# Two chained matrix products with a gelu: zeros from a constant, a cast on two engines, and one matmul moved ahead of two transposes

## The chip, the cores and the metric

The kernel runs on one core of one Trainium2 chip. The metric is the time on the device in microseconds (us); lower is better. A core has TensorE (PE: matrix products and transposes; its weight loads are listed as PEld), VectorE (DVE), ScalarE (ACT) and GpSimd (POOL). SyncE (SP) and POOL also issue transfers (DMA) between HBM and the on-chip memory SBUF. TensorE writes into PSUM, eight banks of 128 partitions x 2 KB. The four runs of the kernel before took 117.74, 118.13, 118.16 and 119.73 us, median 118.15.

## The reference

```python
m, k, n, p = 1024, 1024, 2048, 1024          # all float32
h = np.matmul(a, b)                          # a: m x k, b: k x n
h = 0.5 * h * (1 + np.tanh(np.sqrt(2 / np.pi) * (h + 0.044715 * h ** 3)))
return np.matmul(h, c).astype(np.float32)    # c: n x p
```

## The kernel before, in words

The instructions of each engine stand in the order in which the code writes them; a recording layer adds the waits for data and buffers, per tile. So the order of the calls is the order of the work.

**Data.** `a` is needed with k on the partitions, so it is transposed on TensorE. It is cut into two halves of 512 rows (h = 0 upper, 1 lower) and four quarters of 256 columns of k (q = 0 to 3). A quarter of a half is 128 x 4 x 256 numbers. The upper q = 0 and q = 1 and the lower q = 0 come in float32 over SP into `sta` and are cast to bf16 on the chip (`cast_a` into `ab`, a tile with two buffers). The other five are cast by the transfer itself, which POOL issues (`cast_load_a` into `abq`). `b` is cut into eight slices of 128 rows of k: slices 0 and 1, columns 0 to 511, come in float32 into `stb` and are cast by `cast_b` into `b1`; the rest of `b`, and all of `c`, come over POOL with the cast in the transfer. POOL's first transfer waits for a one-column copy (`gate`, L81) that reads the first quarter of `a`, so its queue starts only when that has landed. POOL issues slices 2 and 3 of `b`, the lower q = 1 of `abq`, the upper q = 2, slices 4 and 5, the lower q = 2, and so on.

**The first product** makes hidden columns 0 to 511 in the plain way, the transposed result in PSUM: bank t (`ps[0, t]`) holds 128 hidden columns by the 512 upper rows, `ps[1, t]` the same for the lower rows. `block(h, tiles, ks)` issues one 128x512 matmul for each slice and tile (L114).

**A turn** (`turn(h, q, bank, ab)`, L136) transposes one quarter of one half: two times four 128x128 transposes into one PSUM bank (L143), each four followed by a VectorE copy into `aT` (L144), which gives the slices 2q and 2q + 1 of that half. It is a generator: each `next(tn)` issues one half of it, so that matmuls can be put between the halves. Both halves lie in one tile `pt`, so the second half's transposes wait until the copy of the first is done. (`turn(1, 0)` alone uses two banks.)

**Stirs** (`stir`, L122) are matmuls of zeros from the tile `warm` into a bank that is overwritten later. They only keep TensorE busy. VectorE sets `warm` to zero at the start (L50). Being float32, each stir is two passes in the trace.

**The order at the start** (L225 to L262): four stirs of 256 columns; the upper q = 0 is cast on VectorE and turned, with a stir of 256 between the halves and one of 128 behind; `cast_b` casts slice 0 in two halves and slice 1, all on ACT; the upper half's matmuls of slice 0 (four) and two of slice 1; `turn(1, 0)`; the two left of slice 1; three matmuls of slice 0 for the lower half (three tiles only, since a bank is needed for the turns); `turn(0, 1)` with three more between its halves. Then for q = 1 and 2 the loop of L249: the upper half's four matmuls of slice 2q and one of slice 2q + 1, the first half of the lower turn `turn(1, q)`, the other three matmuls, its second half; then the lower half's three matmuls, and the upper `turn(0, q + 1)` with three matmuls between its halves. `zero.t1` is a VectorE difference of upper and lower `aT` (one slice at a time here), needed later.

**What follows**, untouched by the change: the gelus (L118, on ACT), three more groups of seven instead of eight block products for the rest of the first product and for the second one (`seven`, L302, its matmuls at L208), and the stores over SP.

Of the kernel before, what the change touches and what calls it, by code (L numbers as in the profile page):

```python
# [9 lines left out]
F32 = mybir.dt.float32  # L10
F32R = mybir.dt.float32r
BF16 = mybir.dt.bfloat16
AF = mybir.ActivationFunctionType
# [6 lines left out]
def kernel(ctx, tc, a, b, c, out):  # L20
    nc = tc.nc
# [3 lines left out]
    H = 512  # L25
# [8 lines left out]
    consts = ctx.enter_context(tc.tile_pool(name="consts", bufs=1))  # L34
# [5 lines left out]
    def slot(tag, shape, dt, name):  # L40
        return big.tile(shape, dt, name=name, tag=tag)

    def bank(i, shape=(128, H), dt=F32, name="ps"):
        return pp.tile(list(shape), dt, name=name, tag=f"bank{i}", padded_shape=None)

    def pieces(tag, bufs, shape, dt, name):
        return small.tile(shape, dt, name=name, tag=tag, bufs=bufs)

    warm = consts.tile([128, 256], F32, name="warm")
    nc.vector.memset(warm, 0.0)  # L50
    ident = consts.tile([128, 128], BF16, name="ident")
    make_identity(nc, ident)
    gate = consts.tile([128, 1], F32, name="gate")
# [7 lines left out]
    b1 = slot("b1", [128, KT, 1024], BF16, "b1")  # L61
# [4 lines left out]
    stb = slot("x0", [128, KT, H], F32, "stb")  # L66
# [39 lines left out]
    def copy(eng, dst, src):  # L106
        if eng is nc.scalar:
            nc.scalar.activation(dst, src, AF.Copy)
        else:
            nc.vector.tensor_copy(dst, src)  # L110

    def mm1(p, t, h, ks):
        for k in ks:
            nc.tensor.matmul(p, b1[:, k, ts(t, 128)], aT[:, h, k],  # L114
                             start=(k == 0), stop=(k == KT - 1))
# [6 lines left out]
    def stir(*widths):  # L122

        for w in widths:
            nc.tensor.matmul(ps[0, 3][:, 0:w], warm[:, 0:128], warm[:, 0:w],
                             start=True, stop=True, skip_group_check=True)

    def cast_a(h, q, *engs):

        ab = pieces("ab", 2, [128, 4, 256], BF16, "ab")  # L130
        for i, eng in enumerate(engs):
            w = 256 // len(engs)
            copy(eng, ab[:, :, ts(i, w)], sta[:, h, q][:, :, ts(i, w)])
        return ab

    def turn(h, q, i, ab):  # L136

        banks = i if isinstance(i, tuple) else (i,)
        pts = [bank(x, (128, 2, H), BF16, "pt") for x in banks]
        for n in range(2):  # L140
            pt = pts[n % len(pts)]
            for m in range(4):
                nc.tensor.transpose(pt[:, n, ts(m, 128)], ab[:, m, ts(n, 128)], ident)  # L143
            nc.vector.tensor_copy(aT[:, h, 2 * q + n], pt[:, n])  # L144
            yield

    def cast_b(k, n=1):
        for i in range(n):
            r = ds(i * (H // n), H // n)
            nc.scalar.activation(b1[:, k, r], stb[:, k, r], AF.Copy)  # L150

    def block(h, tiles, ks):
        for k in ks:
            for t in tiles:
                mm1(ps[h, t], t, h, (k,))
# [56 lines left out]
    def pair(i):  # L212
        x = slot(f"x{i}", [128, 2, 4, H], F32R, "x1")
        return x[:, 0], x[:, 1]
# [3 lines left out]
    def quarters(b, c0, w):  # L218
        return [[b[:, 0:4, ds(c0, w)], b[:, 4:8, ds(c0, w)]],
                [b[:, 0:4, ds(c0 + w, w)], b[:, 4:8, ds(c0 + w, w)]]]  # L220

    zero = Seven(4, quarters(b1, H, 256), BB, [None] * 4, [None] * 4, 2)
    one = Seven(4, quarters(b2, 0, H), BB, [None] * 4, zero.t)

    stir(256, 256, 256, 256)  # L225
    tn = turn(0, 0, 4, cast_a(0, 0, nc.vector))
    next(tn)
    stir(256)
    next(tn)
    stir(128)  # L230
    cast_b(0, 2)
    cast_b(1)
    ab = cast_a(1, 0, nc.vector, nc.scalar)
    block(0, range(4), (0,))
    block(0, range(2), (1,))
    for _ in turn(1, 0, (7, 6), ab):
        pass
    ab = cast_a(0, 1, nc.scalar, nc.scalar)
    block(0, range(2, 4), (1,))
    for t in range(3):  # L240
        ps[1, t] = bank(4 + t)
    zero.t[0], zero.t[1] = pair(2)
    zero.t1(4, 0)
    block(1, range(3), (0,))
    tn = turn(0, 1, 7, ab)
    next(tn)
    block(1, range(3), (1,))
    next(tn)
    for q in range(1, 3):  # L249
        k = 2 * q  # L250
        block(0, range(4), (k,))
        block(0, range(1), (k + 1,))
        tn = turn(1, q, 7, abq[:, q, 1])
        next(tn)
        block(0, range(1, 4), (k + 1,))
        next(tn)
        zero.t1(4, q)
        block(1, range(3), (k,))
        tn = turn(0, q + 1, 7, abq[:, q + 1, 0])
        next(tn)  # L260
        block(1, range(3), (k + 1,))
        next(tn)  # L262
# [221 lines left out]
```

## Time and profile before

| what | us |
|---|---|
| median of four runs | 118.15 |
| the profiled execution's own time | 118.16 |
| its span in the profile | 116.4 |
| PE busy | 111.3 |
| DVE busy | 89.2 |
| ACT busy | 51.8 |
| POOL busy | 17.5 |
| stirs at L125, first start and length of the eight passes | 1.19, 3.77 |
| first transposes (L143) | 5.24 |
| first matmul of a block (L114) | 7.02 |
| first matmul of L208 in the final unbroken run of 400 | 25.16 |

The profile is of one execution. Its span runs from the first to the last recorded instruction; the time of the execution is 1.8 us longer, because of what lies around it. "L125" is line 125 of the kernel before. A busy TensorE is not TensorE at its peak: matmuls are pipelined, and the length of a group includes the drain of its last one, so the pace is read from the starts. In the time line a row is: start, length, engine, line, operation, result and operands, shapes, count, and in brackets the idle time of that engine before it with what ended it. In the chain of waits a row is: start, length, what the end of the program hung on at that time.

### The profile page before, as it was taken

Reading aid. Unit: us, or ns where it says so; the run is one execution under the profiler, and the core shown is the slowest. Engines: PE = TensorE matmul, PEld = TensorE weight load, DVE = VectorE, ACT = ScalarE, POOL = GpSimd, SP = SyncE. Lnnn points to the kernel's source line nnn. Section 1 sums busy time; section 2 is a strip of 40 time slices with the busy share of each in tenths; the row PEclk is TensorE's granted clock in tenths of the full one; section 3 lists DMA queues with packets and bytes.
Section 4 is the critical chain, followed back from the end, with each engine's and each line's share of the span. In section 5 each row is a group of like instructions: output and inputs, shape, how many; then the busy total and the mean of one; then the engine's idle time right before and its main releaser. Section 6 shows DMA issues by size and latency. Waiting matters only on the chain.

```text
span 116.4 us, 1453 instructions
## 1 busy us (share of the span) xinstructions
PE 111.3 (96%) x540; PEld 76.3 (66%) x540; DVE 89.2 (77%) x104; ACT 51.8 (44%) x86; POOL 17.5 (15%) x29
## 2 busy tenths in 40 slices
PE   5999999999999999999999999999999999999980
PEld 4545455545777447888886444588888888888860
DVE  0246356799998999744689999999999986954670
ACT  5063000799369998066699329600033982000000
POOL 2498555222332000000000000000000000000000
PEclk9999999999999999999999999999999999999999
DMA  2999999999999999999000000070000002014993
GB/s 65 307 357 160 200 198 207 201 207 207 206 208 211 212 210 213 210 211 184 8 0 0 0 6 0 2 268 0 0 0 0 0 0 96 0 63 176 367 366 109
DMA packets 13542, 15.81 MB, mean 136 GB/s; under 512 B 736, under 2 KB 9696, under 8 KB 13536
## 3 DMA queue, kind: packets, MB, share of 16 engines
q0 software_dynamic: 8800, 9.44, 48.3%
q1 hardware_dynamic: 4736, 6.29, 15.2%
q8 instruction: 4, 0.07, 0.2%
q14 instruction: 2, 0.02, 0.0%
HBM read 20.97 MB, written 4.19 MB: 216 GB/s over the span
## 4 chain that ended last, share of the span: by engine, by line
PE 86%; DMA 9%; POOL 1%; DVE 0%; issue 0%
PE ps L208 76%; PE ps L114 8%; DMA abq<-in_a_dram 6%; DMA sta<-in_a_dram 3%; PE pt L143 2%; POOL b L89 1%; POOL gate L81 1%; DVE ot L371 0%
## 5 line engine op out<-in xcount | busy, mean ns | idle before, releaser
L208 PE MATMUL ps<-x,s 128*128 128x512 f32 x128 | 29.6, 391 | 0.0
L208 PEld LDWEIGHTS ps<-x,s 128*128 128x128 f32 x128 | 24.0, 188 | 5.1
L208 PE MATMUL ps<-x,x 128*128 128x512 f32 x96 | 22.8, 393 | 0.0
L208 PEld LDWEIGHTS ps<-x,x 128*128 128x128 f32 x96 | 18.0, 188 | 3.9
L114 PE MATMUL ps<-aT,b 128*128 128x512 bf16 x64 | 16.1, 379 | 0.2 <-ACT b L150 0.2
L294 ACT ACTIVATE v<-ps 128x512 f32<-128x512 f32 x10 | 6.0, 599 | 19.5 <-PE ps L208 19.5
L208 PE MATMUL ps<-c_sb,hT 128*128 128x512 bf16 (+1 forms) x72 | 14.2, 356 | 0.0
L208 PE MATMUL ps<-x 128*128 128x512 f32 x56 | 13.2, 392 | 0.0
L144 DVE COPY aT<-pt 128x512 bf16<-128x512 bf16 x16 | 6.7, 423 | 7.0 <-PE pt L143 7.0
L118 ACT ACTIVATE hT<-ps 128x512 bf16<-128x512 f32 x14 | 7.3, 596 | 10.5 <-PE ps L114 10.5
L208 PEld LDWEIGHTS ps<-x 128*128 128x128 f32 x56 | 10.2, 188 | 2.6 <-ACT v L294 0.4
L208 PEld LDWEIGHTS <-hT 128*128 128x128 bf16 x72 | 6.9, 98 | 7.0 <-issue 0.5
L118 ACT ACTIVATE hT<-ot 128x512 bf16<-128x512 f32 x18 | 10.5, 625 | 1.4 <-DVE ot L299 1.2
L208 PE MATMUL ps<-aT,b 128*128 128x512 bf16 x48 | 10.7, 379 | 0.0
L299 DVE TENSOR_TENSOR ot<-ps,v 128x512 f32<-128x512 f32 x10 | 6.7, 687 | 5.2 <-DMA out_dram<-ot 3.8
L299 DVE TENSOR_TENSOR ot<-ps,u 128x512 f32<-128x512 f32 x10 | 6.7, 689 | 5.1 <-ACT u L294 5.1
L166 DVE TENSOR_TENSOR x<-c_sb 128x1024 fp32r<-128x1024 bf16 x8 | 9.2, 1214 | 0.0
L114 PEld LDWEIGHTS <-b 128*128 128x128 bf16 x64 | 5.5, 97 | 4.9 <-ACT b L150 0.9
L208 PEld LDWEIGHTS <-b 128*128 128x128 bf16 x48 | 4.6, 98 | 5.7 <-issue 0.3
L104 POOL DMA_DIRECT2D c_sb<-in_c_dram x8 | 5.7, 712 | 12.5 <-DMA b<-in_b_dram 11.8
L294 ACT ACTIVATE u<-ps 128x512 f32<-128x512 f32 x10 | 5.9, 596 | 3.3 <-PE ps L208 3.2
L166 DVE TENSOR_TENSOR x<-b 128x1024 fp32r<-128x1024 bf16 (+1 forms) x4 | 7.0, 1751 | 0.2 <-issue 0.2
(43 smaller groups left out, 109.5 us busy)
## 6 DMA issues: line engine op xcount, KB each, us to landing
c_sb<-in_c_dram POOLq DMA_DIRECT2D x8, 512.0 KB, 19.7
b<-in_b_dram POOLq DMA_DIRECT2D x6, 512.0 KB, 15.0
out_dram<-ot SPq DMA_DIRECT2D x12, 256.0 KB, 2.1
sta<-in_a_dram SPq DMA_DIRECT2D x3, 512.0 KB, 6.1
abq<-in_a_dram POOLq DMA_DIRECT2D x5, 256.0 KB, 8.5
out_dram<-ot SPq DMA_DIRECT2D x8, 128.0 KB, 2.0
b<-in_b_dram POOLq DMA_DIRECT2D x3, 256.0 KB, 7.9
stb<-in_b_dram SPq DMA_DIRECT2D x1, 512.0 KB, 5.3
```

The source lines that it names most:

```text
L81: nc.gpsimd.tensor_copy(gate, sta[:, 0, 0, 3, 0:1])
L89: nc.gpsimd.dma_start(out=b1[:, 2 * q:2 * q + 2, 0:H], in_=b_part(q))
L104: nc.gpsimd.dma_start(out=c_sb[:, t:t + 2], in_=cv[:, t:t + 2])
L114: nc.tensor.matmul(p, b1[:, k, ts(t, 128)], aT[:, h, k], start=(k == 0), stop=(k == KT - 1))
L118: nc.scalar.activation(hT[h][:, t], p, AF.Gelu_apprx_tanh)
L143: nc.tensor.transpose(pt[:, n, ts(m, 128)], ab[:, m, ts(n, 128)], ident)
L144: nc.vector.tensor_copy(aT[:, h, 2 * q + n], pt[:, n])
L166: nc.vector.tensor_tensor(out=dst[:, r], in0=x[:, r], in1=y[:, r], op=op)
L208: nc.tensor.matmul(p[:, ds(c0, w)], l[:, k, ts(j, 128)], r[:, k, ds(c0, w)], start=(start and k == 0), stop=(k == self.kt - 1), skip_group ...
L294: nc.scalar.activation(st, p, AF.Copy)
L299: nc.vector.tensor_tensor(out=ot, in0=p, in1=st, op=ADD)
```

## The change

The tile `warm` goes; the zeros are a constant that the program's preamble writes into SBUF, one number per partition, read as 128x256 with no step between elements. There are five stirs of 256 at the start instead of four, the one between the halves of the first turn is 128 columns wide instead of 256, and the one behind it 64 instead of 128. `cast_b` takes the engines: slice 0 is cast by halves on VectorE and ACT, with VectorE's half ahead of the copy of the first turn's second half; slice 1 stays on ACT. Three instead of two matmuls of slice 1 stand ahead of `turn(1, 0)`, and one behind it. The upper q = 1 is cast by halves on ACT and VectorE instead of twice on ACT. One matmul of slice 1 for the lower half moves ahead of `turn(0, 1)`. The first `zero.t1` moves behind that turn. In the loop, two instead of one matmul of slice 2q + 1 stand ahead of the lower turn, and two instead of three between its halves. One source line less: lines from L51 on are one lower in the changed kernel until L223.

```diff
-    warm = consts.tile([128, 256], F32, name="warm")
-    nc.vector.memset(warm, 0.0)
+    warm = nc.const_aps.tensor(0.0, [128, 256], F32)
...
-    def cast_b(k, n=1):
-        for i in range(n):
-            r = ds(i * (H // n), H // n)
-            nc.scalar.activation(b1[:, k, r], stb[:, k, r], AF.Copy)
+    def cast_b(k, *engs):
+        w = H // len(engs)
+        for i, eng in enumerate(engs):
+            copy(eng, b1[:, k, ts(i, w)], stb[:, k, ts(i, w)])
...
-    stir(256, 256, 256, 256)
+    stir(256, 256, 256, 256, 256)
     tn = turn(0, 0, 4, cast_a(0, 0, nc.vector))
     next(tn)
-    stir(256)
-    next(tn)
     stir(128)
-    cast_b(0, 2)
-    cast_b(1)
+    cast_b(0, nc.vector, nc.scalar)
+    next(tn)
+    stir(64)
+    cast_b(1, nc.scalar)
     ab = cast_a(1, 0, nc.vector, nc.scalar)
     block(0, range(4), (0,))
-    block(0, range(2), (1,))
+    block(0, range(3), (1,))
     for _ in turn(1, 0, (7, 6), ab):
         pass
-    ab = cast_a(0, 1, nc.scalar, nc.scalar)
-    block(0, range(2, 4), (1,))
+    block(0, (3,), (1,))
+    ab = cast_a(0, 1, nc.scalar, nc.vector)
     for t in range(3):
         ps[1, t] = bank(4 + t)
     zero.t[0], zero.t[1] = pair(2)
+    block(1, range(3), (0,))
+    block(1, range(1), (1,))
+    tn = turn(0, 1, 7, ab)
+    next(tn)
+    block(1, range(1, 3), (1,))
+    next(tn)
     zero.t1(4, 0)
-    block(1, range(3), (0,))
-    tn = turn(0, 1, 7, ab)
-    next(tn)
-    block(1, range(3), (1,))
-    next(tn)
     for q in range(1, 3):
         k = 2 * q
         block(0, range(4), (k,))
-        block(0, range(1), (k + 1,))
+        block(0, range(2), (k + 1,))
         tn = turn(1, q, 7, abq[:, q, 1])
         next(tn)
-        block(0, range(1, 4), (k + 1,))
+        block(0, range(2, 4), (k + 1,))
         next(tn)
         zero.t1(4, q)
```

More of the change, by code (lines that the diff above doesn't have):

```diff
@@ L223 @@
     one = Seven(4, quarters(b2, 0, H), BB, [None] * 4, zero.t)
-    stir(256, 256, 256, 256)
+    stir(256, 256, 256, 256, 256)
     tn = turn(0, 0, 4, cast_a(0, 0, nc.vector))
     next(tn)
-    stir(256)
+    stir(128)
+    cast_b(0, nc.vector, nc.scalar)
     next(tn)
-    stir(128)
-    cast_b(0, 2)
-    cast_b(1)
+    stir(64)
+    cast_b(1, nc.scalar)
     ab = cast_a(1, 0, nc.vector, nc.scalar)
     block(0, range(4), (0,))
-    block(0, range(2), (1,))
+    block(0, range(3), (1,))
     for _ in turn(1, 0, (7, 6), ab):
         pass
-    ab = cast_a(0, 1, nc.scalar, nc.scalar)
-    block(0, range(2, 4), (1,))
+    block(0, (3,), (1,))
+    ab = cast_a(0, 1, nc.scalar, nc.vector)
     for t in range(3):
@@ L242 @@
     zero.t[0], zero.t[1] = pair(2)
-    zero.t1(4, 0)
     block(1, range(3), (0,))
+    block(1, range(1), (1,))
     tn = turn(0, 1, 7, ab)
     next(tn)
-    block(1, range(3), (1,))
+    block(1, range(1, 3), (1,))
     next(tn)
+    zero.t1(4, 0)
     for q in range(1, 3):
```

## The prediction

> **What bounds the kernel now.** I read the busy line first, then the chain of waits, then the time line of the head, engine by engine. The busy line says which engine to follow; TensorE works 96% of the span, so only its idle time can be won and any new idle time of it is lost.
>
> ```profile
> PE 111.3 (96%) x540; PEld 76.3 (66%) x540; DVE 89.2 (77%) x104; ACT 51.8 (44%) x86; POOL 17.5 (15%) x29
> ```
>
> The chain of waits (start, length, what) says from where on that holds. Up to 12.77 us it consists of transfers: the first quarter of `a`, the gate on POOL, then the cast-load of `abq`, issued at 5.99 and landed at 12.73. From there it is TensorE alone until two output additions.
>
> ```profile
> 0.74 3.73 DMA sta<-in_a_dram
> ...
> 5.99 6.73 DMA abq<-in_a_dram
> 12.73 0.05 issue
> 12.77 0.40 PE pt L143 x4
> 13.17 0.65 PE ps L114 x3
> ...
> 25.16 87.99 PE ps L208 x400
> ```
>
> So there are two regions. Ahead of 12.77 an instruction matters only if it makes TensorE come to the transposes of `turn(1, 1)` after the data. Behind 12.77 each idle stretch of TensorE moves the end. The time line of TensorE (start, length, what) shows the border and the two lower turns:
>
> ```profile
> 11.37 1.25 PE L114 MATMUL ps<-aT,b 128*128 128x512 bf16 x5
> 12.77 0.40 PE L143 MATMUL pt<-ident,abq 128*128 128x128 bf16 x4
> 13.01 0.81 PE L114 MATMUL ps<-aT,b 128*128 128x512 bf16 x3
> 13.69 0.38 PE L143 MATMUL pt<-ident,abq 128*128 128x128 bf16 x4
> ...
> 15.74 1.24 PE L114 MATMUL ps<-aT,b 128*128 128x512 bf16 x5
> 16.82 0.39 PE L143 MATMUL pt<-ident,abq 128*128 128x128 bf16 x4
> 17.04 0.81 PE L114 MATMUL ps<-aT,b 128*128 128x512 bf16 x3
> 17.72 0.38 PE L143 MATMUL pt<-ident,abq 128*128 128x128 bf16 x4
> ```
>
> A length includes the drain of the last instruction, so I take spacings: a 128x512 matmul comes every (1.25 - 0.38)/4 = 0.22 us, a transpose every (0.40 - 0.23)/3 = 0.06 us (0.38 and 0.23 are single ones). Five matmuls from 11.37 are issued by 12.46, so TensorE waits 0.31 us for `abq` at 12.77. At 16.82 it doesn't wait: five matmuls from 15.74 end at 16.82. VectorE's copies in the same stretch:
>
> ```profile
> 13.21 0.42 DVE L144 COPY aT<-pt 128x512 bf16<-128x512 bf16 x1 [1.34 <-PE pt L143]
> ...
> 17.24 0.42 DVE L144 COPY aT<-pt 128x512 bf16<-128x512 bf16 x1 [0.88 <-PE pt L143]
> ```
>
> A copy starts 0.42 us after the first transpose of its half turn, lasts 0.42, and the other half's transposes start 0.06 later (both halves share one bank). That is 0.90 us from half to half, whatever TensorE does between.
>
> **The extra matmul ahead of the lower turns.** Today four transposes and three matmuls fill 4 x 0.06 + 3 x 0.22 = 0.88 of those 0.90 us. The edit moves one of the three ahead, which leaves two: 0.66 us of work and 0.24 us of waiting for the copy.
> - *First lower turn (12.77).* The moved matmul runs in the 0.31 us in which TensorE now waits for the transfer; the turn still starts at 12.77 and its second half at 13.69, with the same work behind it. Zero. If that transfer were 0.3 us earlier, the cover would be gone and this turn would cost 0.22 as well.
> - *Second lower turn (16.82).* There is no wait to fill: weights for it could be loaded from 16.75, so the data is there. The turn starts at 16.82 + 0.22 = 17.03, its second half at 17.03 + 0.90 = 17.94 instead of 17.72. **Cost 0.22 us**, on the engine that sets the end. It would be zero if this transfer landed later than 17.03.
> What is late next is everything behind it by the same 0.22: the fourth slices, the gelus, the 400 matmuls from 25.16 on, which wait for nothing from outside; so it reaches the end in full. The move cannot gain: at the start of each second half the same matmuls are done as before. Bounds 0 and 0.43; I take 0.22.
>
> **The zeros from a constant.** VectorE's memset (0.86, 0.27 us) and the wait for it go. SP and ACT issue their first work at 0.73 to 0.74, so TensorE can start at about 0.8 instead of 1.19. Its four 256-wide stirs take 3.77 us, at most 0.94 each; five end between 0.8 + 0.4 + 3.77 = 5.0 (a fifth at full speed) and 0.8 + 4.7 = 5.5. The first transposes are ready at 5.24 (the cast of `ab` ends at 5.18), so they are between 0 and 0.3 late. What hides that: `stb` isn't there before 6.55, and no block can start without it. The constant read with no step between elements is not in the trace; I take the time of the same stirs from `warm`. Memory behind `warm` moves by 1,024 bytes per partition; no row prices that, and I take nothing.
>
> **b's first slice on two engines, and the shorter stirs.** The stirs about the first turn shrink from 256 to 128 and from 128 to 64; they stand in gaps that end with a copy or a cast, so nothing is won by it but idle time. The casts:
>
> ```profile
> 6.55 1.24 ACT L150 ACTIVATE b<-stb 128x256 bf16<-128x256 f32 x3 [4.32 <-DMA stb<-in_b_dram]
> 7.92 0.63 ACT L108 ACTIVATE ab<-sta 128x512 bf16<-128x512 f32 x1
> 7.92 0.52 DVE L110 CAST ab<-sta 128x512 bf16<-128x512 f32 x1 [0.92 <-DMA sta<-in_a_dram]
> ```
>
> ACT does 256 columns in 0.42; VectorE does 512 in 0.52, so 256 between 0.26 and 0.52: I take 0.35. Both halves are ready at about 6.97 (today 6.97 and 7.27), the second slice at 7.5 instead of 7.79. Queued behind VectorE's cast is the copy of the first turn's second half: 6.9 instead of 6.58, done at 7.3; its reader is slice 1, which comes after four matmuls, at 6.97 + 0.88 = 7.85. So seven matmuls run from 6.97 to 8.5, and `turn(1, 0)` starts at 8.49 as today, because its data is cast only then (7.92 + 0.52). One matmul is gained there, and lost again: after that turn one instead of two matmuls stands ahead of slice 0 of the lower half, which waits for a copy until 9.40.
>
> Then the third `ab` has its second half on VectorE: ACT 9.42 to 10.05, VectorE about 9.69 to 10.2; the difference of the lower half starts later, in idle time behind the turn. Four matmuls from 9.40 end at 10.27, `turn(0, 1)` starts then (10.11 today), its second half at 11.18 (11.02), ends 11.40; six matmuls reach 12.70. The data comes at 12.77. **Zero, with 0.07 us left** of what was 0.31.
>
> **Two rules weighed.** *The clock.* The granted clock prints full speed from the start, which the stirs refute: 3.77/8 = 0.47 us per pass at 1.19, 0.65/2 = 0.33 at 5.47. The Trainium skill, "TensorE: Matmul & The Clock Gate" (Part 1: The HAM clock gate), has the clock come up after one busy window of some 3.4 us, and the windows don't start with the kernel. By the row, full speed comes 4.05 us after the first stir at the latest, now at about 4.9: 118.4. By the rule it could come as late as 0.8 + 2 x 3.4 = 7.6; then three matmuls from 6.97 cost 0.22 more each, TensorE comes 0.6 late to `turn(1, 1)`, and the sum is 118.9. I take the row and let the range hold the rule.
>
> *The shared port.* The Trainium skill, "SBUF — State Buffer" (SBUF: two separate sides), says that an fp32 copy on VectorE keeps POOL from writing the descriptors of its transfers. Two casts of 0.35 and 0.52 us now lie beside POOL's issues (5.17 to 11.15), the first beside that of the `abq` that lands at 12.73. If that delay came through, 118.4 + 0.35 = 118.7. But POOL's issues took 1.53 for two beside the cast at 7.92 and 1.50 for two without one, and this transfer spends 6.7 us in flight behind others. I take zero.
>
> **The sum.** 0 (first lower turn) + 0.22 (second) + 0 (head) on the profiled execution: span 116.4 to 116.6, its own time 118.16 to 118.38. Its own time stands 0.01 over the median of the runs, 118.15, so the forecast is **118.4 us**, +0.2%. Under the 0.5% (0.6 us) that a measurement of this kernel can tell from no change.
>
> **Rivals.**
> - *Both copies are covered by transfers* (118.15): the fourth cast-load lands after 17.03, so the second lower turn waits for data in both kernels. For it: TensorE's arrival at 16.82 and the first loading of weights at 16.75 lie within 0.1 us. Against: the landing must slip 0.3. The change then does nothing.
> - *The head comes too late* (119.1; slower): the reserve before 12.77 falls to 0.07, so lateness is paid at once. Place: matmuls from 6.97, at half clock if the gate opens one window (3.4 us) later than in the trace, at about 8.3. Six of the seven then cost 0.22 more, 1.3 us; some 0.6 is taken up by waits on casts and copies, 0.7 is left, and with the 0.22 the time is 119.1. It decides from 0.45 us of lateness on. For it: shorter stirs, 0.3 to 0.4 us idle around the turn. Against: five stirs in a row are longer than today's four.
> - *The head was late in most runs* (117.4; faster): if the usual run comes to 12.77 late by 0.9 or more, the earlier start (0.4), the earlier slice (0.3) and the matmul gained ahead of `turn(1, 0)` (0.22) count; less the 0.22 of the second lower turn that is 0.7 faster. Against: 0.31 us of idle in the profiled run, which took the median time.
>
> **How the numbers follow.** Forecast 0.56, covered 0.14, late head 0.22, faster 0.08. The forecast's own range is 118.0 to 118.7 (its bounds 0 and 0.43, and the 0.1 or 0.2 by which medians differ). The range 117.8 to 119.0 leaves out the far end of the faster and slower cases. Faster by over 0.5%: 0.08. Slower: 0.22 and a little of the forecast's upper end, 0.26. Within: 0.66.
>
> **What would show it.** Right: the first lower turn's transposes within 0.1 us of 12.77 in the same distance to their second half (0.9), TensorE idle some 0.25 us ahead of the second half in both lower turns, the second at about 17.0 and 17.9, the 400 matmuls of L208 from 25.4. Wrong: stirs that still run at 0.47 us per pass behind the first turn, transposes of the first lower turn later than 12.9 with the transfer landed, a landing of `abq` away from 12.73, or 128x512 matmuls with another spacing than 0.22.

## The result, and the profile after

The changed kernel takes 118.48 us (median of 43 runs), the kernel before 118.08 (median of 64 runs measured beside it). The ratio is 1.0034, 95% interval 1.0021 to 1.0047, so +0.25 to +0.55 us: slower, by less than 0.5%. The forecast was 118.4. The ratio leaves out two slow runs of the changed kernel, of 120.55 and 403.25 us.

The busy line of the changed kernel: TensorE is busy a little longer, because there are two more passes of zeros.

```profile
PE 112.0 (96%) x542; PEld 77.3 (66%) x542; DVE 89.4 (77%) x105; ACT 50.9 (44%) x84; POOL 17.5 (15%) x29
```

Its chain of waits (start, length, what) has a new kind of member. Before, TensorE followed the transfers without a break. Now VectorE's copy (L143, L144 before) stands in it twice, once in each lower turn:

```profile
4.99 6.51 DMA b<-in_b_dram
...
11.55 1.47 PE ps L113 x6
13.02 0.35 PE pt L142 x4
13.37 0.02 issue
13.39 0.44 DVE aT L143
13.83 0.04 issue
13.87 0.38 PE pt L142 x4
...
17.38 0.24 PE pt L142 x4
17.61 0.02 issue
17.64 0.43 DVE aT L143
18.07 0.04 issue
18.11 0.38 PE pt L142 x4
...
25.55 87.97 PE ps L207 x400
```

TensorE's time line of the same stretch shows why: six matmuls ahead of each lower turn and two between its halves. The halves still start 0.91 us (12.96 to 13.87) and 0.90 us (17.21 to 18.11) apart.

```profile
11.55 1.47 PE L113 MATMUL ps<-aT,b 128*128 128x512 bf16 x6
12.96 0.40 PE L142 MATMUL pt<-ident,abq 128*128 128x128 bf16 x4
13.19 0.59 PE L113 MATMUL ps<-aT,b 128*128 128x512 bf16 x2
13.87 0.38 PE L142 MATMUL pt<-ident,abq 128*128 128x128 bf16 x4
...
15.92 1.46 PE L113 MATMUL ps<-aT,b 128*128 128x512 bf16 x6
17.21 0.39 PE L142 MATMUL pt<-ident,abq 128*128 128x128 bf16 x4
17.44 0.59 PE L113 MATMUL ps<-aT,b 128*128 128x512 bf16 x2
18.11 0.38 PE L142 MATMUL pt<-ident,abq 128*128 128x128 bf16 x4
```

The chain goes straight from the landing of `b` at 11.50 through six matmuls to the first lower turn at 13.02, because it counts the drain of the last matmul. By the starts, the six are issued by 12.84 (11.55 + 6 x 0.215), and the turn starts at 12.96, 0.05 after the first cast-load of `abq` has landed.

The profiled execution has a span of 116.8 us, 0.4 more than before. It can be taken apart: the first lower turn starts 0.19 later (12.96 against 12.77), and the stretch from its second half to the first matmul of L207 (L208 before) is 11.52 us instead of 11.31, 0.21 more. That first matmul stands in the time lines of before and after at

```profile
25.00 2.32 PE L208 MATMUL ps<-aT,b 128*128 128x512 bf16 x10
25.39 1.89 PE L207 MATMUL ps<-aT,b 128*128 128x512 bf16 x8
```

(the 25.16 and 25.55 of the chains count from the end of the matmul before it). From there on both kernels take 91.4 us. The 0.21 is the second lower turn. The 0.19 is the transfer: the first cast-load of `abq` landed at 12.91 instead of 12.73, and the turn started 0.05 after it in both. Whether the change makes that transfer late, or it was this one execution, only more executions can tell.

### The profile page after: what moved, and what is told of

Same layout as the page of the kernel before. It is cut to its first block, busy times and chain, and to the rows that moved or that the text cites. A ratio compares the mean times of both kernels' runs of the same rounds, so it can differ in the third digit from the quotient of the medians.

```text
span 116.8 us, 1456 instructions
## 1 busy us (share of the span) xinstructions
PE 112.0 (96%) x542; PEld 77.3 (66%) x542; DVE 89.4 (77%) x105; ACT 50.9 (44%) x84; POOL 17.5 (15%) x29
## 3 DMA queue, kind: packets, MB, share of 16 engines
q0 software_dynamic: 8800, 9.44, 48.0%
## 4 chain that ended last, share of the span: by engine, by line
PE 86%; DMA 9%; DVE 1%; POOL 1%; issue 0%
PE ps L207 75%; PE ps L113 9%; DMA b<-in_b_dram 6%; DMA sta<-in_a_dram 3%; PE pt L142 2%; DVE aT L143 1%; POOL gate L80 1%; DVE ot L371 0%
## 5 line engine op out<-in xcount | busy, mean ns | idle before, releaser
L207 PE MATMUL ps<-x,s 128*128 128x512 f32 x128 | 29.6, 391 | 0.0
L207 PEld LDWEIGHTS ps<-x,s 128*128 128x128 f32 x128 | 24.0, 188 | 5.1
L207 PE MATMUL ps<-x,x 128*128 128x512 f32 x96 | 22.9, 394 | 0.0
L207 PEld LDWEIGHTS ps<-x,x 128*128 128x128 f32 x96 | 18.0, 188 | 3.9
L207 PE MATMUL ps<-c_sb,hT 128*128 128x512 bf16 (+1 forms) x72 | 14.2, 356 | 0.0
L207 PE MATMUL ps<-x 128*128 128x512 f32 x56 | 13.2, 392 | 0.0
L207 PEld LDWEIGHTS ps<-x 128*128 128x128 f32 x56 | 10.2, 188 | 2.6 <-ACT u L294 0.4
L143 DVE COPY aT<-pt 128x512 bf16<-128x512 bf16 x16 | 6.7, 422 | 6.9 <-PE pt L142 6.9
L207 PEld LDWEIGHTS <-hT 128*128 128x128 bf16 x72 | 6.9, 98 | 7.0 <-issue 0.5
L207 PE MATMUL ps<-aT,b 128*128 128x512 bf16 x48 | 10.7, 379 | 0.0
L207 PEld LDWEIGHTS <-b 128*128 128x128 bf16 x48 | 4.6, 98 | 5.7 <-issue 0.3
```

Of the source, the lines that this page charges most:

```text
L207: nc.tensor.matmul(p[:, ds(c0, w)], l[:, k, ts(j, 128)], r[:, k, ds(c0, w)], start=(start and k == 0), stop=(k == self.kt - 1), skip_group ...
```

## The experiments

Two theories were to be told apart. *The turns*: the loss is made by the matmuls moved ahead of turns, 0.22 us wherever TensorE and not a transfer starts the turn. *The head*: the casts that are now on VectorE delay POOL's transfers, and with them everything.

Each timed round compares with fresh runs of the kernel before. One experiment was that kernel against itself:

> The kernel before, unchanged, measured against itself. Ratio 1.000 within 0.1%; its floor at 117.5 to 117.6 us as in the other rounds. What it differs by is the noise under which differences of 0.1 to 0.2 us in the other rounds can't be read from medians. If the cast-load of abq lands early in its profiled execution (before 12.2 us), the first lower turn should start at about 12.15; if late, 0.05 us after the landing.

It gave 118.33 against 118.06, ratio 1.0022 (0.9998 to 1.0046), where 0.1% had been expected. So with 22 runs against 27 a median can't settle 0.2 us. Two other readings are finer. The distances inside one trace repeat within 0.03 us. And the fastest fifth of a kernel's runs has a steady mean: 117.68 to 117.69 for the kernel before in every round, 117.72 for this control. It says nothing of the long executions, and of 22 runs it is four.

| kernel | median, beside before (us) | ratio (95%) | fastest fifth, over before (us, from rounded means) |
|---|---|---|---|
| changed | 118.48, 118.08 | 1.0034 (1.0021 to 1.0047) | +0.48 |
| loop's edit only | 118.32, 117.99 | 1.0022 (1.0002 to 1.0042) | +0.38 |
| changed, loop's edit undone | 118.22, 117.99 | 1.0027 (1.0002 to 1.0051) | +0.07 |
| first lower turn only | 118.19, 117.99 | 1.0015 (0.9996 to 1.0035) | +0.13 |
| second lower turn only | 118.24, 117.99 | 1.0013 (0.9995 to 1.0031) | +0.17 |
| three ahead | 118.68, 118.14 | 1.0050 (1.0029 to 1.0071) | +0.78 |
| changed, no moves | 118.29, 118.14 | 1.0010 (0.9987 to 1.0033) | +0.02 |
| first upper move only | 117.95, 118.14 | 0.9988 (0.9965 to 1.0012) | +0.08 |
| none ahead | 118.20, 118.14 | 0.9999 (0.9971 to 1.0027) | -0.02 |
| before against itself | 118.33, 118.06 | 1.0022 (0.9998 to 1.0046) | +0.04 |

What each one's profiled execution shows (us; "landed" is the end of the first cast-load of `abq`, read from the trace's landings; the last column is the way from the second half of the first lower turn to the first matmul of L208):

| kernel | landed | first lower turn starts | second half | way to L208 | span |
|---|---|---|---|---|---|
| before | 12.73 | 12.77 | 13.69 | 11.31 | 116.4 |
| before, again | 12.82 | 12.87 | 13.78 | 11.31 | 116.5 |
| changed | 12.91 | 12.96 | 13.87 | 11.52 | 116.8 |
| loop's edit only | 12.23 | 12.66 | 13.56 | 11.53 | 116.5 |
| changed, loop's edit undone | 12.12 | 12.33 | 13.23 | 11.31 | 115.9 |
| first lower turn only | 12.12 | 12.36 | 13.26 | 11.31 | 116.0 |
| second lower turn only | 12.67 | 12.72 | 13.63 | 11.52 | 116.6 |
| three ahead | 13.21 | 13.38 | 14.28 | 11.74 | 117.4 |
| changed, no moves | 12.83 | 12.88 | 13.79 | 11.30 | 116.5 |
| first upper move only | 13.09 | 13.13 | 14.04 | 11.31 | 116.7 |
| none ahead | 12.46 | 12.51 | 13.61 | 11.28 | 116.3 |

Two things are read from this table at once. The landing moves by 1.1 us from execution to execution, 12.12 to 13.21, in no order that follows the edits. And the last column depends on nothing but the second lower turn: 11.3 without a matmul moved there, 11.5 with one, 11.74 with two.

**The loop's edit, alone and left out.**

```diff
-        block(0, range(1), (k + 1,))
+        block(0, range(2), (k + 1,))
         tn = turn(1, q, 7, abq[:, q, 1])
         next(tn)
-        block(0, range(1, 4), (k + 1,))
+        block(0, range(2, 4), (k + 1,))
```

> The kernel before with only the edit of the loop (one more matmul ahead of both lower turns). If the lower turns alone carry the loss: +0.22 us (second turn) to +0.43 us (both, in executions whose first cast-load of abq lands early), TensorE idle some 0.25 us ahead of the second half of each lower turn. If the head carries part of it (0.18 us by later landings of POOL's transfers): +0.22 us and landings as in the kernel before, so less than the whole change.

> The whole change without the edit of the loop. If the lower turns alone carry the loss: the time of the kernel before, within 0.1 us. If the head delays POOL's transfers: +0.18 us, with slices 2 and 3 of b landing at 11.5 instead of 11.3. If the head was late in most runs before: a gain, up to 0.7 us.

Put into the kernel before, the edit alone gives a ratio of 1.0022, and +0.38 in the fastest fifth, near the 0.43 of both turns. Its profiled execution was one with an early landing, so it shows what the trace of before could not:

```profile
11.58 1.24 PE L114 MATMUL ps<-aT,b 128*128 128x512 bf16 x5
12.66 0.39 PE L143 MATMUL pt<-ident,abq 128*128 128x128 bf16 x4
12.88 0.59 PE L114 MATMUL ps<-aT,b 128*128 128x512 bf16 x2
13.56 0.38 PE L143 MATMUL pt<-ident,abq 128*128 128x128 bf16 x4
```

(One record of the six matmuls is missing; by the 0.22 between matmuls it started at 11.36.) The data landed at 12.23, TensorE came at 12.66: here it is TensorE that starts the first lower turn, and the moved matmul makes it later by its full 0.22.

The changed kernel without the loop's edit was measured at 1.0027, which by itself would speak for the head. But the control gave almost as much, the fastest fifth gives +0.07, and the traces speak against the head's theory as it was put: with the casts on VectorE the first cast-load landed at 12.91, 12.12 and 12.83 in the three kernels of the table that have them, within the 12.12 to 13.21 of the eight that don't. Six of this kernel's 22 runs took 119.0 us or more, five of them in a row, against two of the 75 beside it; no trace shows such an execution, so what made them long stays open. What this kernel's own trace does show of the head is a smaller thing of the other kind. The upper turn of the second quarter, ahead of which the change also moves a matmul, starts at 10.13 with two matmuls between its halves:

```profile
9.35 0.63 ACT L107 ACTIVATE ab<-sta 128x512 bf16<-128x512 f32 x1 [0.87 <-DMA sta<-in_a_dram]
10.03 0.31 PEld L142 LDWEIGHTS <-ab 128*128 128x128 bf16 x4 [0.23 <-ACT ab L107]
10.13 0.39 PE L142 MATMUL pt<-ident,ab 128*128 128x128 bf16 x4
10.35 0.59 PE L113 MATMUL ps<-aT,b 128*128 128x512 bf16 x2
11.03 0.38 PE L142 MATMUL pt<-ident,ab 128*128 128x128 bf16 x4
11.47 1.03 PE L113 MATMUL ps<-aT,b 128*128 128x512 bf16 x4
12.33 0.39 PE L142 MATMUL pt<-ident,abq 128*128 128x128 bf16 x4
```

Again 0.90 us from half to half, and TensorE comes to the first lower turn at 12.33, after the data (12.12). The price of this move is smaller than 0.22: without it the upper turn would have waited for the cast of `ab` until 10.03, so the moved matmul makes it only 0.10 late.

**One lower turn at a time.** The same edit, with `2 if q == 1 else 1` and `2 if q == 2 else 1` in place of 2.

> The kernel before with one more matmul ahead of the first lower turn alone. If a transfer starts that turn in the usual execution: 0. If TensorE comes after the data in the usual execution: +0.22 us.

> The kernel before with one more matmul ahead of the second lower turn alone. If TensorE starts that turn, as the trace of before says: +0.22 us (four transposes and two matmuls are 0.66 us, the copy takes 0.90). If its cast-load usually lands after 17.0 us: 0.

Both ratios lie between the two expectations (1.0015 and 1.0013, or +0.18 and +0.15 us, with intervals down to 0.9995), and don't decide. The traces do. The second turn costs 0.21 in the last column (11.52 against 11.31), with its data there 0.3 us ahead of the turn. The first turn, in an execution that landed at 12.12, started at 12.36; without the moved matmul TensorE would have come at 12.14 and the data at 12.17, so here it cost 0.2. In the fastest fifths the two are +0.13 and +0.17, and both together +0.38.

**The edit doubled, and turned round.** `range(3)` ahead and `range(3, 4)` between; then nothing ahead and `range(4)` between.

> Two more matmuls ahead of both lower turns (three of the four), one left between the halves: the edit of the loop doubled. If the wait for the copy (0.90 us from half to half) sets the price: 4 x 0.06 + 0.22 = 0.44 us of work and 0.46 of waiting at each lower turn, +0.43 at the second one and +0.12 (late landing) to +0.43 (early landing) at the first: +0.55 to +0.87 us, twice the loop's edit or a little more. If instead the landing of the cast-loads sets the turns: about the same time as the edit of the loop alone (+0.3).

> The opposite of the edit: no matmul of slice 2q + 1 ahead of the lower turns, all four between the halves. Four transposes and four matmuls are 1.10 us, over the 0.90 of the copy, so TensorE waits for no copy there: -0.03 us at each lower turn in executions with an early landing; where the first lower turn's cast-load lands late, up to +0.2 us, since one matmul less lies ahead of the wait for it. In the median 0 to +0.1 us; a gain of over 0.1 would say that the waiting in the kernel before is larger than read.

Three ahead: 1.0050, +0.54 in the median and +0.78 in the fastest fifth, about twice the single edit, as the wait for the copy demands. The trace names the waiting; with one matmul left, VectorE's copy ends it:

```profile
13.38 0.39 PE L143 MATMUL pt<-ident,abq 128*128 128x128 bf16 x4
13.60 0.38 PE L114 MATMUL ps<-aT,b 128*128 128x512 bf16 x1
14.28 0.38 PE L143 MATMUL pt<-ident,abq 128*128 128x128 bf16 x4 [0.30 <-DVE aT L144]
```

The halves are 0.90 apart with one, two and three matmuls between them, and 1.10 with four. None ahead is equal to the kernel before (0.9999): TensorE then waits for no copy, and the waits that this takes away were 0.03 us each.

**The head without its moves.** The changed kernel with the order of the kernel before at the upper turn and in the loop; constant zeros, stirs, casts and the third matmul of slice 1 are left.

```diff
-    block(1, range(1), (1,))
     tn = turn(0, 1, 7, ab)
     next(tn)
-    block(1, range(1, 3), (1,))
+    block(1, range(3), (1,))
...
-        block(0, range(2), (k + 1,))
+        block(0, range(1), (k + 1,))
...
-        block(0, range(2, 4), (k + 1,))
+        block(0, range(1, 4), (k + 1,))
```

> The whole change without the moves: neither the matmul ahead of the lower turns nor the one ahead of the upper turn of the second quarter; what is left are the constant zeros, the stirs, the casts, and one matmul of slice 1 ahead of the first lower turn. If those are free and the moves carry all of the loss: the time of the kernel before, within 0.1 us, its fastest executions too (117.5). If the head's casts or stirs cost something: +0.1 to +0.2 us.

1.0010 (0.9987 to 1.0033), +0.02 in the fastest fifth: free, as far as this can be measured, and no gain either. Three of its 22 runs took 119.0 us or more, against two of the 59 beside it.

**The move ahead of the upper turn alone,** in the kernel before.

```diff
+    block(1, range(1), (1,))
     tn = turn(0, 1, 7, ab)
     next(tn)
-    block(1, range(3), (1,))
+    block(1, range(1, 3), (1,))
```

> The kernel before with one matmul of slice 1 (lower half) ahead of the upper turn of the second quarter alone. If the same 0.90 us from half to half holds there and TensorE starts the first lower turn in the usual execution: up to +0.22 us in executions in which slices 2 and 3 of b land before 11.1 us, zero in those in which they land at 11.3 or later; in the median about +0.1.

0.9988 (0.9965 to 1.0012): the expected +0.1 didn't show. In its profiled execution the data landed at 13.09, where the move costs nothing; the fastest fifth has +0.08, nearer the 0.10 read above than 0.22. What this move costs on average stays open.

**Late transfers in every execution.** POOL's gate reads SP's last load of `a` instead of the first, alone and with one lower turn's edit each.

```diff
-    nc.gpsimd.tensor_copy(gate, sta[:, 0, 0, 3, 0:1])
+    nc.gpsimd.tensor_copy(gate, sta[:, 0, 1, 3, 0:1])
```

> The kernel before with POOL's gate on the last of SP's loads of a (landing at 9.3 us) instead of the first (4.5), so that all cast-loads land later, in every execution. Slower than before by what the first lower turn's data is late, 0.5 to 3 us; this is the base for the next two.

> The same late gate, and one more matmul ahead of the first lower turn alone. If the price of the edit at that turn is taken by the wait for the transfer: no difference from the late gate alone (within 0.1 us), where the same edit with the early gate gave about +0.2. If the edit costs at that turn in any case: +0.22 us over the late gate alone.

> The same late gate, and one more matmul ahead of the second lower turn alone. The two cast-loads lie 4.0 us apart and TensorE needs 4.04 us from turn to turn, so the second turn is TensorE's with a late queue too: +0.22 us over the late gate alone. If with a late queue the second turn waits for its transfer as well: 0.

Medians 123.05, 122.86 and 123.54 of six runs each, which spread over 1.6 to 3.9 us: inconclusive for differences of 0.2. The edit was too coarse, and cost more than the 0.5 to 3 us expected. After TensorE's long wait its clock falls (the granted clock is 0.50 from 16.1 to 19.4 us, 1.00 before and after), and the first lower turn is then slow for another reason. From the trace of the late gate alone:

```profile
14.44 1.03 PE L114 MATMUL ps<-aT,b 128*128 128x512 bf16 x4 [3.14 <-DMA b<-in_b_dram]
16.59 0.61 PE L143 MATMUL pt<-ident,abq 128*128 128x128 bf16 x4 [1.12 <-DMA abq<-in_a_dram]
16.99 1.48 PE L114 MATMUL ps<-aT,b 128*128 128x512 bf16 x3
...
19.71 0.39 PE L143 MATMUL pt<-ident,abq 128*128 128x128 bf16 x4
```

Four transposes take 0.61 instead of 0.39, three matmuls 1.48 instead of 0.81. So nothing is learned of the first lower turn, and a milder delay was not tried. The second lower turn comes when the clock is full again, and there the traces do tell: from the second half of the upper turn ahead of it to the first matmul of L208 it is 9.47 us with the late gate alone (20.61 to 30.08), 9.47 with the first turn's edit and 9.69 with the second's (19.54 to 29.23). That is the +0.22 expected.

## Why the prediction was right, step by step

- **The second lower turn, 0.22: right.** It measured 0.21 to 0.22 in the changed kernel, in the loop's edit alone and in this turn's edit alone, and 0.43 for two matmuls. Its cast-load had landed at 16.91 when the turn started at 17.21, so the rival in which both copies are covered by transfers falls here, but narrowly. Without the moved matmul TensorE would have come at 16.99, and the data could be used from 16.96 (0.05 after the landing). In the eleven traces with the early gate the two cast-loads land 3.95 to 4.00 us apart, and unless this turn was edited TensorE takes 4.03 to 4.04 us from turn to turn, so this small lead of the data repeats.
- **The first lower turn, zero: right for the execution it was read from, too small for the others.** With the landing at 12.91 the turn cost nothing, as forecast: 0.05 us after the data, 0.91 to the second half. Two of the signs that the prediction named came out against it (12.96 for the transposes instead of within 0.1 of 12.77, 12.91 for the landing instead of 12.73), because they took that landing for fixed; the distances held. But the landing is no constant. Of eleven profiled executions with the early gate, eight landed at 12.46 or later and three at 12.12 to 12.23, and in those three TensorE came after the data. (It did so in a late one too, with three matmuls ahead: seven matmuls from 11.86 last to 13.37, and the data had landed at 13.21.) The prediction gave this case its price ("this turn would cost 0.22 as well") and kept it in the bound of 0.43, but took the end of the bounds that one execution showed. When slices 2 and 3 of `b` land so late that TensorE waits for them, the cast-load of `abq` follows 1.3 to 1.4 us behind, and six matmuls (1.29 us) fit in between; when they land early, TensorE starts its six later than the landing, and there is nothing to cover the sixth.
- **The head, zero: right for the casts, stirs and constant zeros as far as measured; not always for the move ahead of the upper turn.** The head of the changed kernel ran close to the figures forecast: stirs from 0.78, the first cast of slice 0 in 0.29 (0.35 taken), the upper turn at 10.21 and 11.11 (10.27 and 11.18). "Zero, with 0.07 us left" holds when the data comes at 12.77. When it comes at 12.12 the upper turn's moved matmul makes TensorE late (12.33), by 0.10, since the rest of the matmul runs while the cast of `ab` is awaited anyway. The rival of a gain (117.4) falls with the kernel without the moves, which is no faster than the one before. What is open is the long executions: two kernels with this head and the old loop had nine of 44 runs at 119.0 us or more, against four of the 134 runs beside them, and whether the head makes such executions more frequent was not tested.
- **The sum.** +0.22 was worked out (118.15 to 118.37, given as 118.4); measured +0.40, and the 0.22 lies just outside the interval of 0.25 to 0.55. That 118.48 came so near 118.4 is in part luck: the kernel before took 0.07 less than its first four runs had it, and the loss was 0.18 more. The term that was too small is the first lower turn, and with it the upper turn: zero in most executions, 0.2 and 0.1 in those that land early. Three such in eleven add only about 0.1 to the mean, so some 0.1 us of the 0.40 is not accounted for; the control shows that a median of this kernel can be off by more than that. The 0.19 by which the profiled execution's transfer was later is not counted as part of it: landings scatter by 1.1 us. That a change must reach 0.5% to be told from none was too strict: with 43 and 64 runs the interval is 0.13% to either side.
- **The rule of the clock.** The reading that the prediction took from the trace would have given full speed at about 4.9. In the changed kernel's trace the first three of the four transposes at 5.17 still came 0.1 us apart, the last 0.06 behind, and the four took 0.48 us. Eight of the eleven traces have the stirs of the kernel before: in five of them the first four transposes took 0.40 us, in three 0.61, at half the pace. In one of these (none ahead) the next four were at half clock too:

```profile
4.99 0.61 PE L143 MATMUL pt<-ident,ab 128*128 128x128 bf16 x4
5.39 1.17 PE L125 MATMUL ps<-warm 128*128 128x256 f32 x2
6.35 0.63 PE L143 MATMUL pt<-ident,ab 128*128 128x128 bf16 x4
6.78 0.60 PE L125 MATMUL ps<-warm 128*128 128x128 f32 x2
7.22 1.46 PE L114 MATMUL ps<-aT,b 128*128 128x512 bf16 x6
8.51 0.28 PE L143 MATMUL pt<-ident,ab 128*128 128x128 bf16 x2
```

  So the same start gets its full clock at different times. This agrees with the Trainium skill, "TensorE: Matmul & The Clock Gate" (Part 1: The HAM clock gate), where the window that lets the clock come up doesn't begin with the kernel. This execution was at full speed for the matmuls at 7.22 and met the lower turn of the first quarter at 8.51, where the profile of before had 8.49; it took 118.08 us. So a full clock that comes after 6.35 instead of by 5.24 is hidden in the head, and the late-head rival (some 119.1) would need one that is later still; none was seen. (The prediction's 0.47 us per pass takes in the drain; from the second pass on they start 0.43 apart.)
- **The rule of the shared port.** POOL's issue of the first two cast-loads, before (no cast on VectorE beside it) and after (VectorE's new cast of `b` beside it):

```profile
5.99 1.50 POOL L86 DMA_DIRECT2D abq<-in_a_dram  x2
...
5.82 1.51 POOL L85 DMA_DIRECT2D abq<-in_a_dram  x2
6.57 0.29 DVE L109 CAST b<-stb 128x256 bf16<-128x256 f32 x1 [0.45 <-DMA stb<-in_b_dram]
```

  The next two took 1.53 us before and 1.54 after, both beside the cast at 7.92, and one of the two earliest landings (12.12) came with the new casts in place. By the Trainium skill, "SBUF — State Buffer" (SBUF: two separate sides), an fp32 copy on VectorE can keep POOL from writing the descriptors of its transfers; of such a delay, for which the prediction had reckoned 0.35 us, these issues show no more than 0.01.

## What to carry to other kernels

Work that stands between two dependent steps of another engine is not idle filling: here four transposes and three matmuls filled 0.88 of the 0.90 us that a copy takes, and each one moved ahead cost its own 0.22 us at the second lower turn, while the hole it could fill at the first existed only when a transfer was late. Before moving work into a wait, count what is left where it came from. And when a stretch is bounded by the landing of a transfer, look at several executions: the landing may scatter by more than the edit is worth, so that the same edit is free in one execution and costs its full price in the next.

## What was not expected

The first cast-load that POOL issues, slices 2 and 3 of `b`, landed between 10.74 and 11.81 us in eleven executions whose transfers up to then were alike (SP's last load landed between 9.11 and 9.44). The next one follows it by 1.3 to 1.4 us each time, so this one transfer sets the start of the first lower turn in most executions, and with it a part of the time's scatter. What makes it fast or slow was not found. And in each of the three kernels with the late gate, a wait of TensorE of 3.1 to 3.4 us for slices 2 and 3 of `b` went with a stretch at half clock (granted clock 0.50) of at least 3.3 us, which began in one of them before the wait had ended.
